# A hybrid attention layer on one core: the first gate-up product on the token halves' difference moved ahead of the last tile's differences, and a shorter chain for the inverse norms

## The chip, the core and the metric

The kernel runs on one core of a Trainium2 chip. The metric is the device time of one execution in microseconds (us), the median of several executions. The engines are named as in the profile: PE multiplies matrices, with its weight loads shown apart as PEld; DVE, ACT and POOL work elementwise; SP issues the DMAs. Each engine takes its instructions in the order in which they stand in its queue.

## What is computed

The program is one layer: a norm and an input projection, two kinds of attention side by side (NSA heads and HGRN2 heads), an output projection with the residual, then a second norm and a SwiGLU feed-forward block. The change touches the seam between the output projection and the feed-forward block:

```python
x = x + mix @ w_out[l]
h = rms_norm(x, norm_ffn[l])
gate, up = jnp.split(h @ w_gate_up[l], 2, axis=-1)
x = x + (jax.nn.silu(gate) * up) @ w_down[l]
```

There are 1024 tokens, in eight tiles of 128, and 1024 features; the feed-forward block is 2816 wide.

## The kernel before

Each float32 product is made of three matmuls: both operands are split in a high part (a copy on ACT, line 111) and a low part (a subtraction on DVE, line 112), and lines 118 to 120 multiply high by high, high by low and low by high. `product` splits one operand, a 128x512 page of weights, and runs the twelve matmuls against an `operand` that stands ready.

An `operand` tile is made by four transposes on PE into one PSUM bank (line 724), a copy on ACT (line 727) and a subtraction on DVE (line 728). The banks of these tiles come from `bank_s`, which has four: the fifth tile's transposes wait until DVE has read the first.

The gate-up stage multiplies by a scheme with seven block products in place of eight. Tokens are in two halves (tiles 0 to 3 and 4 to 7), features in two halves, gate and up columns in two. The scheme needs sums and differences of blocks. For the tokens, `pair_a(t)` makes the operands `b22` and `t1o` (`t1o` is the difference of the halves, already subtracted by line 748, and for the last tile by line 981), `pair_d(t)` makes three further differences `d` (lines 987 to 989, on POOL, the first of the last tile on DVE), and `pair_b(t)` turns them into the operands `t2o`, `t3o` and `t4o`. For the weights of block f, `gate_up_s1` adds two pages, `s1 = a[1,0] + a[1,1]` (line 972, POOL), and takes a difference (line 973, POOL); `gate_up_b` multiplies `s1` by `t1o` (the product `q`), subtracts a page from `s1` (line 1012, POOL) and multiplies it by `t2o`, and so on through the pages; a further subtraction on POOL (line 1015) makes the page of its last product. `gate_up_a(0)` and `gate_up_a(1)`, the first two blocks' products on `b11` and `b21`, run ahead of that. The weight pages come by DMA through a ring of three slots of two pages each (`rpage`, line 708).

Before this seam the last output tile (token tile 7) is added to the residual (line 497), its squares are summed on ACT (line 242), and `norm_stats` makes the inverse root on DVE through `rsqrt` (lines 125 to 131): twelve instructions on a 128x1 column. Then line 743 scales x of tile 7. The other seven tiles went the same way earlier, during the attention stage.

The order of the instructions on each engine isn't the order of the code. A scheduler sets it when the program is built: of the instructions that its own model of the times holds ready it takes the one that stands first in the code. Two lines that change places in the code thus change who goes first where both are held ready, also on engines that the edit doesn't name, and another number of instructions on one engine can shift the interleaving from there on.

Of the kernel before, what the change touches and what calls it, by code (L numbers as in the profile page):

```python
# [8 lines left out]
F32 = mybir.dt.float32  # L9
F32R = mybir.dt.float32r  # L10
BF16 = mybir.dt.bfloat16
I32 = mybir.dt.int32
U8 = mybir.dt.uint8
AF = mybir.ActivationFunctionType
OP = mybir.AluOpType
# [3 lines left out]
P = 128  # L19
D = 1024  # L20
T = 1024
NT = T // P
# [10 lines left out]
EPS = 1e-6  # L33
# [15 lines left out]
def hybrid_layer(ctx: ExitStack, tc: tile.TileContext, x, x_t, par, w_in, k_norm, pos_k, pos_v,  # L49
                 ck_w1, ck_w2, cv_w1, cv_w2, w_out, norm_ffn, w_gu, w_down, cst, hmask, out):  # L50
    nc = tc.nc
    V, A, G, PE = nc.vector, nc.scalar, nc.gpsimd, nc.tensor

    const = ctx.enter_context(tc.tile_pool(name="const", bufs=1))
    small = ctx.enter_context(tc.tile_pool(name="small", bufs=2))
# [19 lines left out]
    def bank8():  # L75

        turn[0] = (turn[0] + 1) % 8
        return acc() if turn[0] < 2 else ps_t() if turn[0] < 4 else bank_s()
# [6 lines left out]
    def bank_s():  # L85
        return pool[0].tile([P, 512], F32, name="bank", tag="s", bufs=4)
# [21 lines left out]
    def split(hi, lo, src, gain=None):  # L108

        if gain is None:  # L110
            A.activation(hi, src, AF.Copy)  # L111
            V.tensor_tensor(lo, src, hi.bitcast(F32), op=OP.subtract)  # L112
        else:
            A.activation(hi, src, AF.Copy, scale=gain)
            V.scalar_tensor_tensor(lo, src, gain, hi.bitcast(F32), op0=OP.mult, op1=OP.subtract)

    def mm3(o, ah, al, bh, bl, first, last, chained=False):
        PE.matmul(o, ah, bh, start=first, stop=False, skip_group_check=chained)  # L118
        PE.matmul(o, ah, bl, start=False, stop=False, skip_group_check=chained)  # L119
        PE.matmul(o, al, bh, start=False, stop=last, skip_group_check=chained)  # L120

    def rsqrt(y, ss, n, scale, eps, parts=P):
        v = small.tile([P, 64], F32, name="rs_v", tag="rs_v")[:parts, :n]
        t = small.tile([P, 64], F32, name="rs_t", tag="rs_t")[:parts, :n]
        V.tensor_scalar(v, ss, scale, eps, op0=OP.mult, op1=OP.add)
        V.tensor_scalar(t.bitcast(I32), v.bitcast(I32), 1, None, op0=OP.logical_shift_right)
        V.tensor_scalar(y.bitcast(I32), t.bitcast(I32), -1, 0x5F3759DF, op0=OP.mult, op1=OP.add)
        for _ in range(3):
            V.tensor_tensor(t, y, y, op=OP.mult)
            V.scalar_tensor_tensor(t, t, -0.5, v, op0=OP.mult, op1=OP.mult)  # L130
            V.scalar_tensor_tensor(y, t, 1.5, y, op0=OP.add, op1=OP.mult)
# [105 lines left out]
        return lambda i: parts_of(f(i))  # L237

    def norm_stats(src, junk):
        ss = small.tile([P, 1], F32, name="n_ss", tag="n_ss")  # L240
        rs = small.tile([P, 1], F32, name="n_rs", tag="n_rs", bufs=NT)
        A.activation(junk, src, AF.Square, accum_out=ss)
        rsqrt(rs, ss, 1, 1.0 / D, EPS)
        return rs

# [463 lines left out]
    def product(src, op, w=None, o=None):  # L711
        o = bank8() if o is None else o
        w = wring.tile([P, 2, 512], F32R, name="wop", tag="w") if w is None else w
        split(w[:, 0], w[:, 1], src)
        for c in range(4):
            sl = slice(c * P, (c + 1) * P)
            mm3(o, w[:, 0, sl], w[:, 1, sl], op[:, 0, c], op[:, 1, c], c == 0, c == 3)
        return o
# [231 lines left out]
    b21, t2o, b22, t1o, t3o, t4o = (opA[:, 0], opA[:, 1], opB[:, 0], opB[:, 1], opC[:, 0], opC[:, 1])  # L950
# [18 lines left out]
    def gate_up_s1(f, a):  # L969

        s1 = tmp[:, 8 + f % 2] if f else ff.tile([P, 512], F32, name="s1", tag="d", bufs=6)
        G.tensor_tensor(s1, a[1, 0], a[1, 1], op=OP.add)  # L972
        G.tensor_tensor(a[1, 0], a[0, 0], a[1, 0], op=OP.subtract)
        return s1
# [3 lines left out]
    def pair_a(t):  # L978
        operand(b22, x1[:, t + 4, 512:1024], t, bank_s)
        if t == 3:  # L980
            V.tensor_tensor(x1[:, 7, 0:512], x1[:, 7, 0:512], x1[:, 3, 0:512], op=OP.subtract)
        operand(t1o, x1[:, t + 4, 0:512], t, bank_s)

    def pair_d(t):
        xa, xb = x1[:, t, :], x1[:, t + 4, :]
        d = dif[t] = [ff.tile([P, 512], F32, name=f"d{i}", tag="d", bufs=6) for i in range(3)]
        (G if t < 3 else V).tensor_tensor(d[0], xb[:, 512:1024], xb[:, 0:512], op=OP.subtract)
        G.tensor_tensor(d[1], d[0], xa[:, 0:512], op=OP.subtract)
        G.tensor_tensor(d[2], xa[:, 512:1024], d[0], op=OP.subtract)

    def pair_b(t):
        for i, op in enumerate((t2o, t3o, t4o)):
            operand(op, dif[t][i], t, bank_s)
# [3 lines left out]
    nxt = [gate_up_a(0), gate_up_a(1)]  # L997
    for t in range(3):
        pair_a(t)
    for t in range(3):  # L1000
        pair_d(t)
        pair_b(t)
    s1s = [gate_up_s1(0, nxt[0][0])]
    pair_a(3)
    pair_d(3)
    pair_b(3)
    tmp = big.tile([P, 16, 512], F32, name="tmp", tag="A1")

    def gate_up_b(f, a, s1):
        u2, c11, u3, c22 = (tmp[:, 4 * (f % 2) + i] for i in range(4))  # L1010
        q = product(s1, t1o)
        G.tensor_tensor(s1, s1, a[0, 0], op=OP.subtract)  # L1012
        V.tensor_tensor(u2, product(s1, t2o), u2, op=OP.add)
        act_later()
        G.tensor_tensor(a[0, 1], a[0, 1], s1, op=OP.subtract)
        V.tensor_tensor(u3, product(a[1, 0], t3o), u2, op=OP.add)
        act_later()
        V.tensor_tensor(c22, q, u3, op=OP.add)
        V.tensor_tensor(u2, q, u2, op=OP.add)
        V.tensor_tensor(u3, product(a[1, 1], t4o), u3, op=OP.add)  # L1020
        act_later()
        V.tensor_tensor(u2, product(a[0, 1], b22), u2, op=OP.add)
        act_later()
        i, kh = f // 2, f % 2
        for hf, (gt, up) in enumerate(((c11, u3), (u2, c22))):
            th = ff.tile([P, 512], F32, name="th", tag="d", bufs=6) if kh else tmp[:, 10 + 2 * (i % 2) + hf]
            A.activation(th, gt, AF.Tanh, scale=0.5)
            V.scalar_tensor_tensor(th, th, 1.0, gt, op0=OP.add, op1=OP.mult)
            V.scalar_tensor_tensor(th, th, 0.5, up, op0=OP.mult, op1=OP.mult)
            if (kh, hf) != (0, 1):  # L1030
                act_store({(0, 0): 0, (1, 0): 1, (1, 1): 5}[kh, hf], i, th)
            blk[kh, hf] = th
        if kh:
            later.extend(act_sums(i, dict(blk)))
# [5 lines left out]
    def act_store(k, i, src):  # L1040
        nc.sync.dma_start(act_d[(k * NH + i) * P:(k * NH + i + 1) * P, :], src)
# [27 lines left out]
    def act_later():  # L1069
        if later:  # L1070
            later.pop(0)()
# [214 lines left out]
```

## Time and profile before

| what | value |
|---|---|
| median of 3 runs | 1405.82 us (1403.95 to 1405.95) |
| the profiled execution | 1406.47 us, its span 1404.6 us |
| PE busy | 1371.6 us, 98% of the span |
| DVE busy | 1048.0 us, 75% |
| ACT busy | 596.5 us, 42% |
| POOL busy | 392.1 us, 28% |

The profiled execution is 0.65 us above the median. The span runs from the first to the last instruction; the rest of the time lies around it. PE's busy time counts overlapping, pipelined matmuls, so a busy PE isn't PE at its peak. Times of single instructions are counted from the start of the span. The attention stage ends near 750 us, the seam lies between 750 and 780 us, gate-up runs to about 1235 us, and the down projection to the end.

### The profile page before, as it was taken

To read this page: it belongs to the slowest core of one execution; us is meant where nothing else is said; L and a number is where in the kernel's file an instruction comes from. 1 tells how busy PE (TensorE), PEld (TensorE's weight loads), DVE (VectorE), ACT (ScalarE), POOL (GpSimd) and SP (SyncE) were. 2 spreads that over 40 slices of the span, in tenths; PEclk is the share of its full clock that TensorE was granted. 3 is DMA by queue.
4 is the path that set the end of the run, shared out by engine and by line. 5 is a ranking of instruction groups with operands and counts; after the bars stand their busy time and mean duration, and the time that the engine had idled before them with its cause. 6 is when DMAs were issued, how large, how long until landed. Compare 5 with 4: busy or idle time off the path is not lost.

```text
span 1404.6 us, 19716 instructions
## 1 busy us (share of the span) xinstructions
PE 1371.6 (98%) x7092; PEld 1129.5 (80%) x7092; DVE 1048.0 (75%) x1893; ACT 596.5 (42%) x1153; POOL 392.1 (28%) x341
## 2 busy tenths in 40 slices
PE   9999999999999999999998999999999999999998
PEld 7888888989977777777776888888888888887787
DVE  5317888626788888888877888888888887689764
ACT  7323333323446666566654433333333333443332
POOL 0001111010044442344436433233233230158400
PEclk9999999999999999999999999999999999999999
DMA  8411110111220001000003333333333328887521
GB/s 324 127 45 31 31 31 28 54 31 46 94 88 1 1 1 61 31 16 31 16 16 105 96 101 97 112 98 113 113 112 99 106 98 294 327 300 269 171 97 55
DMA packets 108769, 135.72 MB, mean 97 GB/s; under 512 B 6112, under 2 KB 63872, under 8 KB 108672
## 3 DMA queue, kind: packets, MB, share of 16 engines
q1 hardware_dynamic: 108672, 134.46, 28.7%
q8 instruction: 56, 0.92, 0.3%
q14 instruction: 41, 0.34, 0.1%
HBM read 105.87 MB, written 28.57 MB: 96 GB/s over the span
## 4 chain that ended last, share of the span: by engine, by line
PE 82%; DVE 12%; ACT 2%; issue 2%; POOL 1%; DMA 1%; SPq 0%; ACTq 0%; POOLq 0%; DVEq 0%
PE bank L118 9%; PE bank L119 9%; PE bank L120 9%; PE a L118 8%; PE a L120 8%; PE a L119 8%; PE ps_t L119 4%; PE ps_t L120 4%; PE ps_t L118 4%; PE ps_t L861 3%; PE a L865 2%; DVE wop L112 2%; PE a L866 2%; PE ps_t L375 1%; PE ps_s L839 1%
## 5 line engine op out<-in xcount | busy, mean ns | idle before, releaser
L850 POOL TENSOR_SCALAR pbig<-pbig,den,gates 128x640 f32<-128x640 f32 (+7 forms) x128 | 103.9, 816 | 166.9 <-DVE den L849 146.9
L111 ACT ACTIVATE wop<-rpage 128x512 fp32r<-128x512 f32 x132 | 82.7, 630 | 156.9 <-PE bank L120 70.7
L112 DVE TENSOR_TENSOR wop<-rpage,wop 128x512 fp32r<-128x512 f32 x132 | 100.7, 765 | 14.6 <-ACT wop L111 12.7
L864 DVE TENSOR_TENSOR ph<-ps_t,ph 128x512 fp32r<-128x512 f32 x126 | 84.3, 683 | 18.5 <-ACT ph L863 17.6
L863 ACT ACTIVATE ph<-ps_t 128x512 fp32r<-128x512 f32 x126 | 72.7, 596 | 49.6 <-PE ps_t L861 39.7
L381 POOL TENSOR_TENSOR kp<-kp,fp 128x256 f32<-128x256 f32 x28 | 20.3, 725 | 232.8 <-PE bank L358 181.3
L861 PE MATMUL ps_t<-ident,pbig 128*128 128x128 f32 x504 | 78.7, 275 | 2.1 <-POOL pbig L850 2.1
L112 DVE TENSOR_TENSOR wop<-act_a,wop 128x512 fp32r<-128x512 f32 x48 | 46.8, 976 | 33.1 <-ACT wop L111 33.1
L861 PEld LDWEIGHTS ps_t<-ident,pbig 128*128 128x128 f32 x504 | 61.0, 141 | 11.9 <-POOL pbig L850 3.2
L1012 POOL TENSOR_TENSOR tmp<-tmp,rpage 128x512 f32<-128x512 f32 x21 | 31.3, 1488 | 140.6 <-DVE wop L112 140.6
L112 DVE TENSOR_TENSOR wlo<-wraw,whi 128x1024 fp32r<-128x1024 f32 (+2 forms) x27 | 32.0, 1188 | 46.0 <-PE a L120 19.3
L848 ACT ACTIVATE pbig<-ps_s,nm 128x640 f32<-128x640 f32 (+3 forms) x64 | 55.9, 875 | 24.1 <-DVE nm L847 19.0
L111 ACT ACTIVATE wop<-act_a 128x512 fp32r<-128x512 f32 x48 | 30.3, 631 | 82.8 <-PE bank L120 58.0
L118 PE MATMUL bank<-wop 128*128 128x512 f32 x165 | 65.3, 396 | 0.1
L119 PE MATMUL bank<-wop 128*128 128x512 f32 x165 | 65.2, 395 | 0.0
L120 PE MATMUL bank<-wop 128*128 128x512 f32 x165 | 65.1, 394 | 0.0
L847 DVE TENSOR_REDUCE nm<-ps_s 128x1 f32<-128x640 f32 (+3 forms) x64 | 58.1, 913 | 4.7 <-PE ps_s L842 3.0
L865 PE MATMUL a<-ph,kv 128*128 128x512 f32 x132 | 58.8, 445 | 2.2 <-ACT ph L863 1.4
L866 PE MATMUL a<-ph,kv 128*128 128x512 f32 x132 | 57.5, 436 | 2.9 <-DVE ph L864 1.8
L112 DVE TENSOR_TENSOR wop<-tmp,wop 128x512 fp32r<-128x512 f32 x42 | 43.6, 1039 | 20.6 <-ACT wop L111 19.9
L972 POOL TENSOR_TENSOR tmp<-rpage 128x512 f32<-128x512 f32 x20 | 26.1, 1306 | 115.2 <-DMA rpage<-in_w_gate_up_dram 115.2
L111 ACT ACTIVATE wop<-tmp 128x512 fp32r<-128x512 f32 x42 | 26.6, 633 | 70.2 <-POOL tmp L1012 37.5
(458 smaller groups left out, 4454.2 us busy)
## 6 DMA issues: line engine op xcount, KB each, us to landing
rpage<-in_w_gate_up_dram SPq DMA_DIRECT2D x86, 256.0 KB, 3.1
raws<-in_w_down_dram SPq DMA_DIRECT2D x35, 512.0 KB, 7.5
act_a<-act_d SPq DMA_DIRECT2D x12, 1024.0 KB, 6.4
act_d<-as SPq DMA_DIRECT2D x33, 256.0 KB, 2.2
act_e<-act_d SPq DMA_DIRECT2D x6, 1024.0 KB, 7.6
act_d<-tmp SPq DMA_DIRECT2D x22, 256.0 KB, 2.1
act_d<-th SPq DMA_DIRECT2D x22, 256.0 KB, 2.1
xn<-in_x_dram SPq DMA_DIRECT2D x8, 512.0 KB, 5.5
```

The source lines that it names most:

```text
L111: A.activation(hi, src, AF.Copy)
L112: V.tensor_tensor(lo, src, hi.bitcast(F32), op=OP.subtract)
L118: PE.matmul(o, ah, bh, start=first, stop=False, skip_group_check=chained)
L119: PE.matmul(o, ah, bl, start=False, stop=False, skip_group_check=chained)
L120: PE.matmul(o, al, bh, start=False, stop=last, skip_group_check=chained)
L847: V.tensor_reduce(nm, sv, axis=AX.XY, op=OP.max, negate=True)
L850: G.tensor_scalar(pp, pp, den, gates[:, qb, h * 3 + 1 + b:h * 3 + 2 + b], op0=OP.mult, op1=OP.mult)
L861: PE.transpose(pt[:, r * P:(r + 1) * P], wts[r][:, c0:c0 + P], ident)
L863: A.activation(ph[:, 0], pt, AF.Copy)
L864: V.tensor_tensor(ph[:, 1], pt, ph[:, 0].bitcast(F32), op=OP.subtract)
L865: PE.matmul(o, vst[b][:, kb, g, :], ph[:, 0], start=b == 0 and kb == kb0, stop=False)
L866: PE.matmul(o, vst[b][:, kb, g, :], ph[:, 1], start=False, stop=False)
```

## The change

Two edits. In `norm_stats` the chain is written out with the factor -0.5 taken into a column `h` once, so that one round of the iteration is two instructions in place of three: ten instructions in place of twelve, with four small tiles. In the seam, `gate_up_s1(0)` stands ahead of the loop over `pair_d` and `pair_b` instead of behind it, and the product `q` of block 0 is issued between `pair_d(3)` and `pair_b(3)`, into a bank of `bank_s`; `gate_up_b` takes it from there.

```diff
     def norm_stats(src, junk):
-        ss = small.tile([P, 1], F32, name="n_ss", tag="n_ss")
-        rs = small.tile([P, 1], F32, name="n_rs", tag="n_rs", bufs=NT)
+        ss, v, h, t = (small.tile([P, 1], F32, name=n, tag=n) for n in ("n_ss", "n_v", "n_h", "n_t"))
+        y = small.tile([P, 1], F32, name="n_rs", tag="n_rs", bufs=NT)
         A.activation(junk, src, AF.Square, accum_out=ss)
-        rsqrt(rs, ss, 1, 1.0 / D, EPS)
-        return rs
+        V.tensor_scalar(v, ss, 1.0 / D, EPS, op0=OP.mult, op1=OP.add)
+        V.tensor_scalar(t.bitcast(I32), v.bitcast(I32), 1, None, op0=OP.logical_shift_right)
+        V.tensor_scalar(y.bitcast(I32), t.bitcast(I32), -1, 0x5F3759DF, op0=OP.mult, op1=OP.add)
+        V.tensor_scalar(h, v, -0.5, None, op0=OP.mult)
+        for _ in range(3):
+            V.scalar_tensor_tensor(t, y, y, h, op0=OP.mult, op1=OP.mult)
+            V.scalar_tensor_tensor(y, t, 1.5, y, op0=OP.add, op1=OP.mult)
+        return y
...
     for t in range(3):
         pair_a(t)
+    s1s = [gate_up_s1(0, nxt[0][0])]
     for t in range(3):
         pair_d(t)
         pair_b(t)
-    s1s = [gate_up_s1(0, nxt[0][0])]
     pair_a(3)
     pair_d(3)
+    q_first = [product(s1s[0], t1o, o=bank_s())]
     pair_b(3)
...
-        q = product(s1, t1o)
+        q = q_first.pop() if q_first else product(s1, t1o)
```

The diff moves more than its lines. Behind the edit each line of the code stands six or seven lines lower: 972 is 978, 987 to 989 are 993 to 995, 1012 is 1019, 727 is 733, 724 is 730.

On POOL, at the seam, before (`s_7716` is `s1`, the `d` are the differences of `pair_d`, three for each tile):

```order
L987 TENSOR_TENSOR d_7635<-x_3322 128x512
L988 TENSOR_TENSOR d_7636<-d_7635,x_3322 128x512
L989 TENSOR_TENSOR d_7637<-x_3322,d_7635 128x512
L987 TENSOR_TENSOR d_7662<-x_3322 128x512
L988 TENSOR_TENSOR d_7663<-d_7662,x_3322 128x512
L989 TENSOR_TENSOR d_7664<-x_3322,d_7662 128x512
L987 TENSOR_TENSOR d_7689<-x_3322 128x512
L988 TENSOR_TENSOR d_7690<-d_7689,x_3322 128x512
L989 TENSOR_TENSOR d_7691<-x_3322,d_7689 128x512
L972 TENSOR_TENSOR s_7716<-rpage 128x512
```

And now, the first ten on POOL at the same place:

```order
L978 TENSOR_TENSOR s_7627<-rpage 128x512
L993 TENSOR_TENSOR d_7630<-x_3322 128x512
L979 TENSOR_TENSOR rpage<-rpage 128x512
L994 TENSOR_TENSOR d_7631<-d_7630,x_3322 128x512
L995 TENSOR_TENSOR d_7632<-x_3322,d_7630 128x512
L993 TENSOR_TENSOR d_7657<-x_3322 128x512
L1019 TENSOR_TENSOR s_7627<-s_7627,rpage 128x512
L994 TENSOR_TENSOR d_7658<-d_7657,x_3322 128x512
L1022 TENSOR_TENSOR rpage<-rpage,s_7627 128x512
L995 TENSOR_TENSOR d_7659<-x_3322,d_7657 128x512
```

The sum of the two weight pages went from the tenth place to the first, and the other three instructions on block 0's weights stand between the differences; the three differences of tile 2 and the last two of tile 3 follow as eleventh to fifteenth.

On ACT, behind the copies of the operand tiles of `pair_a(0)` to `pair_a(2)`, before (`wop` is the split of a weight page, line 111; `opA` and `opC` are operand tiles, line 727):

```order
L727 ACTIVATE opB<-bank 128x4x128 x6
L727 ACTIVATE opA<-bank 128x4x128
L727 ACTIVATE opC<-bank 128x4x128 x2
L111 ACTIVATE wop<-rpage 128x512
L111 ACTIVATE wop<-epage 128x512
L727 ACTIVATE opA<-bank 128x4x128
L111 ACTIVATE wop<-s_7716 128x512
L727 ACTIVATE opC<-bank 128x4x128 x2
```

And now:

```order
L733 ACTIVATE opB<-bank 128x4x128 x6
L111 ACTIVATE wop<-rpage 128x512
L111 ACTIVATE wop<-epage 128x512
L111 ACTIVATE wop<-s_7627 128x512 x2
L111 ACTIVATE wop<-rpage 128x512 x3
L733 ACTIVATE opA<-bank 128x4x128
L733 ACTIVATE opC<-bank 128x4x128 x2
```

All seven splits of block 0's and block 1's first pages stand ahead of the first copy of a difference tile; on DVE the subtractions stand in the same order. The second split of `s` reads what line 1019 writes, and the last of the three `rpage` reads what line 1022 writes.

On PE, behind the 32 transposes of `b21`, `b22` and `t1o`, before came five tiles of differences, then the 24 matmuls of the first two blocks. Now it reads, from the end of those 24:

```order
L120 MATMUL a_7569<-opA,wop 128x512
L730 MATMUL bank<-ident,d_7630 128x128 x4
L730 MATMUL bank<-ident,d_7631 128x128 x4
L730 MATMUL bank<-ident,d_7632 128x128 x4
L730 MATMUL bank<-ident,d_7657 128x128 x4
L730 MATMUL bank<-ident,d_7658 128x128 x4
L730 MATMUL bank<-ident,d_7659 128x128 x4
L730 MATMUL bank<-ident,d_7684 128x128 x4
L730 MATMUL bank<-ident,d_7685 128x128 x4
L730 MATMUL bank<-ident,d_7686 128x128 x4
L730 MATMUL bank<-ident,x_3322 128x128 x8
L118 MATMUL bank<-opB,wop 128x512
```

The 24 matmuls come first and all nine tiles of differences after them, then the two tiles of `pair_a(3)` and the twelve matmuls of `q`; behind these stand the three tiles of `pair_b(3)`, and then seven matmuls of the product on `b22`, ahead of the product on `t2o`.

## Rows read from the trace of the kernel before

**Rows 1.** Busy time by stretch: PE, PEld, DVE, ACT, POOL (instructions), clock, DMA share, GB/s.

```profile
750.00:760.00 10.00, 6.55 (x47) 4.64 (x44) 9.21 (x21) 8.30 (x16) 7.75 (x7) 1.00 0.76 210
760.00:770.00 10.00, 8.61 (x45) 6.62 (x46) 9.85 (x15) 3.12 (x8) 5.09 (x4) 1.00 0.18 52
770.00:780.00 10.00, 8.40 (x45) 6.59 (x46) 8.40 (x15) 7.72 (x16) 6.44 (x6) 1.00 0.01 3
...
850.00:950.00 100.00, 100.00 (x443) 82.83 (x442) 81.99 (x103) 32.23 (x53) 30.48 (x21) 1.00 0.31 96
```

**Rows 2.** PE in time order at the seam: start, us, [idle before <- releaser].

```profile
753.25 0.63 PE L724 MATMUL bank<-ident,x 128*128 128x128 f32 x4 [0.90 <-DVE opA L728]
...
767.86 1.91 PE L724 MATMUL bank<-ident,d 128*128 128x128 f32 x16
...
772.76 0.66 PE L724 MATMUL bank<-ident,d 128*128 128x128 f32 x4 [1.03 <-POOL d L988]
773.99 0.66 PE L724 MATMUL bank<-ident,d 128*128 128x128 f32 x4 [0.57 <-POOL d L989]
774.40 0.47 PE L118 MATMUL bank<-opB,wop 128*128 128x512 f32 x1
```

**Rows 3.** POOL in time order at the seam.

```profile
747.01 1.31 POOL L987 TENSOR_TENSOR d<-x 128x512 f32<-128x512 f32 x1
...
753.46 1.27 POOL L989 TENSOR_TENSOR d<-x,d 128x512 f32<-128x512 f32 x1
...
760.63 1.29 POOL L972 TENSOR_TENSOR s<-rpage 128x512 f32<-128x512 f32 x1
...
768.52 1.59 POOL L1012 TENSOR_TENSOR s<-s,rpage 128x512 f32<-128x512 f32 x1 [4.83 <-DVE wop L112]
...
772.65 1.28 POOL L989 TENSOR_TENSOR d<-x,d 128x512 f32<-128x512 f32 x1
```

**Rows 4.** The weight pages of block 0: first issue, time to landing, DMA by stretch.

```profile
751.46 0.74 SPq L708 DMA_DIRECT2D rpage<-in_w_gate_up_dram  x1
...
rpage<-in_w_gate_up_dram SPq DMA_DIRECT2D x4, 256.0 KB, 5.8
...
758.00:759.00 1.00, 0.26 (x4) 0.17 (x3) 1.00 (x3) 0.87 (x3) 0.92 (x2) 1.00 0.90 222
759.00:760.00 1.00, 0.48 (x4) 0.25 (x3) 1.00 (x3) 1.00 (x3) 1.00 (x2) 1.00 0.01 2
```

**Rows 5.** DVE: the chain's last instructions by tile (min/median/max ns), and two tiles' subtractions.

```profile
L131 DVE SCALAR_TENSOR_TENSOR n_rs<-rs_t,n_rs x24: 141/159/973, 590.8 to 761.2; 128x1 f32<-128x1 f32 x24
...
770.33 1.28 DVE L728 TENSOR_TENSOR opC<-bank,opC 128x512 fp32r<-128x512 f32 x2
```

**Rows 6.** ACT in time order: the first two splits of weight pages.

```profile
758.87 0.63 ACT L111 ACTIVATE wop<-rpage 128x512 fp32r<-128x512 f32 x1
759.40 0.61 ACT L111 ACTIVATE wop<-epage 128x512 fp32r<-128x512 f32 x1
```

**Rows 7.** Two stretches in which the granted clock (third value from the right) fell.

```profile
561.00:562.00 1.00, 0.72 (x3) 0.72 (x4) 1.00 (x2) 0.23 (x2) 0.37 (x1) 0.78 0.00 0
...
564.00:565.00 1.00, 1.00 (x6) 0.82 (x5) 1.00 (x2) 0.00 (x0) 0.75 (x1) 0.51 0.00 0
...
1302.00:1303.00 1.00, 0.00 (x0) 0.00 (x0) 1.00 (x2) 0.00 (x0) 1.00 (x2) 0.63 0.63 37
...
1309.00:1310.00 1.00, 1.00 (x5) 0.81 (x5) 0.67 (x1) 0.00 (x0) 0.00 (x0) 0.96 0.38 143
```

**Rows 8.** PE's waits by releaser (total, times, longest): 590 to 746, then 780 on.

```profile
PE ps_s L839 <- ACT pbig L848: 2.0, 3, 0.7
PE a L866 <- DVE ph L864: 1.8, 5, 0.4
PE a L866 <- DVE rs_t L129: 0.6, 1, 0.6
...
PE ps_t L119 <- DVE wop L112: 3.5, 4, 2.4
```

## The prediction, made before the changed kernel ran

> **What bounds the kernel now.** I read the busy time by stretch first. PE is busy 98% of the span, and through gate-up it never waits: 443 matmuls in 100 us, 0.226 us each, from 850 to 950 us, and the next two stretches of that length read alike [rows 1]. The seam is different. Between 750 and 780 us PE is idle for 30 - 6.55 - 8.61 - 8.40 = 6.4 us, while DVE is nearly full [rows 1]. PE's own rows say why. In the first part its transposes wait for a bank that DVE has to empty (0.90 us at 753.25); at the end they wait for POOL's last two differences, 1.03 and 0.57 us; from 774.40 on it runs through [rows 2]. So what the seam gains or loses reaches the end in full, unless the later stages take some of it up.
>
> **The sum of the weight pages at the head of POOL's queue.** This decides the forecast. Before, POOL began the differences at 747.01, right behind its work for the last tiles, and came to the sum at 760.63 [rows 3]. Now the sum is POOL's first instruction there, and it needs two pages of block 0. Their DMAs are not moved: the first of four is issued at 751.46, the four take 5.8 us in the median, and the DMA engines are at 0.90 from 758 to 759 us and at 0.01 in the next microsecond [rows 4]. So the last of these pages lands near 759.0. POOL, which has work at 747, stands until then, with fourteen instructions behind the sum. Its pace is 1.29 us: from 747.01 to 753.46 are five of them [rows 3]. I count from 759.0: the first, second, sixth, seventh, ninth and thirteenth end at 760.3, 761.6, 766.7, 768.0, 770.6 and 775.8.
>
> PE comes to it as follows. The 32 transposes end near 755.4, as before. Then stand the 24 matmuls, whose first page ACT can split only when it has landed; before, the two splits started at 758.87 and 759.40 [rows 6]. So PE starts them near 758.9 and, at 0.226 us each, ends near 764.5. Four tiles of differences follow, as POOL makes them, to 767.2 (the fourth is POOL's sixth instruction). The fifth needs a bank. No bank is emptied, since ACT and DVE hold the splits ahead of the tiles' copies: the second split of s waits for POOL's seventh, and the last of the three pages for POOL's ninth, at 770.6. That split ends at 771.2, the first copy at 771.8, and DVE empties the first bank by 772.4. **PE thus stands from about 767 to 772.5.**
>
> From there DVE empties a tile in 0.60 to 0.64 us [rows 5]. Nine tiles from 771.8 would be done at 777.3, but the ninth is POOL's thirteenth (775.8): transposes to 776.3 (16 take 1.91 us, so four about half a microsecond [rows 2]), copy to 776.9, subtraction to 777.5. The two tiles of pair_a(3) behind it are ready at 778.6, and q's twelve matmuls run to 781.3. The first difference of tile 3 is made on DVE by 779.2, the other two on POOL by 781.9, their transposes end at 782.4. The same work was done before at 774.40 + 12 x 0.226 = 777.1 [rows 2]: before, q's matmuls were the last of it. **The term is 782.4 - 777.1 = +5.3 us.** What the edit is built on is there: q's 2.7 us do cover POOL's two differences of tile 3, on which PE waited 1.6 us. But they are covered five microseconds later. If POOL ran at the 1.59 us that line 1012 took [rows 3], the twelve instructions from the second to the thirteenth would add up to 12 x 0.30 = 3.6 us; DVE has little to do while POOL catches up, so I add nothing and leave part of this to the range.
>
> **A second wait behind it.** After that point PE has seven matmuls of the b22 product (1.6 us, to 784.0), and then needs the t2o tile of tile 3. Its copy on ACT stands behind a split of block 1's s, which waits for POOL's sixteenth instruction: 781.9 + 1.3 = 783.2, split to 783.8, a tanh to 784.3, the copy to 784.9, DVE to 785.5. **+1.5 us**; it is nothing if POOL and ACT make up that time, so its bounds are 0 and 1.5.
>
> **The clock.** After PE's waits near 560 us the granted clock is under 1 in four slices of a microsecond, from 0.78 to 0.51, and around the wait at 1300 to 1303 us in eight, from 0.63 to 0.96, with 0.50 between [rows 7]. That is the lower level, 1.2 of 2.4 GHz. The work done there at half speed, some 3.2 and 6.9 us, cost 1.6 and 3.4 us. In the seam of before the clock held at 1.00, with PE busy 6.55 of 10 us [rows 1]. Now PE has a gap without any work of 3.4 us and one of over 5; the wait before the fall at 1302 us was 2.4 us [rows 8]. What the first costs is hidden, since PE has to wait at 767 anyway. After the second come q and what follows. I take the cheaper incident, **+1.6 us**, since the sparse transposes from 772 on may raise the clock again ahead of q; bounds 0 and 3.4. The Trainium skill ("TensorE: Matmul & The Clock Gate", Part 1: The HAM clock gate) says that an idle PE drops to 1.2 GHz and sustained activity lets it back, which the two places of this trace agree with. By it alone the term would be of the dearer kind, as the gap is longer than either, and the time 1.8 us higher.
>
> **The shorter chain.** Two instructions of twelve go, for each of eight tiles, and POOL stands while the last chain runs. One such instruction takes 159 ns in the median and up to 973 [rows 5]. For tile 7 the chain and the scaling behind it end near 758.5 instead of 764.8, but nobody waits for that: the transposes of tile 7 stand behind all differences on PE. I count nothing for it here. In the attention stage DVE saves 7 x 2 instructions, some 2 us, off the path but for the 0.6 us that PE waited there for the chain [rows 8]. The order of the whole stage from about 590 us on is shuffled, though; PE's waits in it are 2.0 + 1.8 + 0.6 = 4.4 us [rows 8], and I take -0.6, with -4.4 and +4.4 as bounds.
>
> **The sum**: 5.3 + 1.5 + 1.6 - 0.6 = +7.8 us. On the profiled execution's 1406.47 us that is 1414.3; it is 0.65 us above the median of the runs, so the forecast is 1413.6 us, 0.55% slower. All bounds together are +0.9 and +14.6 (1406.7 and 1420.4).
>
> **Rivals.** *It does what its name says.* If the pages were there when POOL reaches the sum, the differences would be made as early as before, q would fill PE's 1.6 us, and with the shorter chain half of the other 4.8 us of PE's idle time in the seam could go: -4.0 us, 1401.8. It decides by the landing: the sum would have to start 6.8 us sooner than 759.0, at 752, for the change to cost nothing. Against it: the first of the four DMAs is issued only at 751.46 [rows 4]. Chance 0.06.
>
> *The loss is given back.* From 1290 to 1310 us PE waits 3.5 us for DVE's splits [rows 8], and the half clock costs another 3.4 [rows 7]. If that stage is set by DMAs and POOL and not by when PE comes, a PE that is late waits less: 1413.6 - 6.9 = 1406.7, no change. For it: DVE and POOL have their own queue there. Against it: their pages come through slots that gate-up frees, so they are late as well. Chance 0.10.
>
> *The shuffled attention stage* costs as much again as PE's waits in it, 4.4 us, instead of 0.6 less: 1413.6 + 5.0 = 1418.6. For it: the scheduler's model also let the sum go first. Chance 0.09.
>
> **How the numbers follow.** The forecast has 0.75, from 1409 to 1418. A measurement of this kernel can tell about 0.2% (2.8 us) from no change. The first rival is faster, the second within that, the forecast and the third slower: 0.06, 0.10, 0.84. The range of 1408.0 to 1418.8 leaves out the first two rivals and little else.
>
> **What would show it.** In the trace of after: POOL idle from about 747 to 759 us, released by the DMA of a weight page, and the differences only then; ACT's second split of s released by line 1019; PE with a gap of about five microseconds that ends with DVE's first difference tile; q's matmuls near 778.6 instead of 774.4; the clock at 0.5 around there. I am wrong if POOL's sum starts before 752 us, if the copies of difference tiles go ahead of the splits, or if PE's later waits shrink by what the seam loses.

## The result: 1.4% slower, more than twice the forecast loss

The changed kernel takes 1423.76 us in the median of four runs (1422.99 to 1424.61), the kernel before 1404.88 (1403.46 to 1405.95). The ratio is 1.0143, with an interval of 1.0131 to 1.0155: about 19 to 20 us lost where 7.8 were forecast. At the seam the sign and the mechanism were right and the size was not; the attention stage, forecast to gain a little, lost. 1423.76 lies 5 us above the end of the range.

The busy time by stretch shows where PE stands now; it answers to [rows 1] (the columns are those named there).

```profile
750.00:760.00 10.00, 8.12 (x53) 6.34 (x51) 7.33 (x19) 6.46 (x12) 0.27 (x1) 1.00 0.62 172
760.00:770.00 10.00, 6.14 (x17) 4.87 (x18) 7.07 (x9) 1.78 (x3) 5.53 (x4) 0.66 0.51 145
770.00:780.00 10.00, 3.85 (x25) 3.01 (x23) 4.71 (x4) 4.15 (x8) 9.92 (x8) 0.95 0.05 15
780.00:790.00 10.00, 6.57 (x33) 5.88 (x34) 8.93 (x13) 3.99 (x8) 4.00 (x4) 0.71 0.30 90
790.00:800.00 10.00, 7.31 (x37) 5.68 (x36) 5.86 (x7) 4.27 (x9) 9.84 (x8) 1.00 0.01 2
850.00:950.00 100.00, 100.00 (x443) 82.81 (x442) 84.99 (x107) 32.21 (x52) 29.30 (x20) 1.00 0.33 107
```

Between 760 and 780 us PE is busy 10 of 20 us, and it is not through with the seam before 800. POOL, which was busy 7.75 us of 750 to 760 before [rows 1], is busy 0.27 us there now. Gate-up behind it is untouched: 443 matmuls in 100 us, as before. PE's own rows say for what it waits (start, us, [idle before <- releaser]), to be held against [rows 2]:

```profile
757.32 2.02 PE L730 MATMUL bank<-ident,x 128*128 128x128 f32 x12 [0.89 <-DVE n_t L248]
763.86 0.80 PE L118 MATMUL a<-opA,wop 128*128 128x512 f32 x1 [4.52 <-ACT wop L111]
...
773.42 0.66 PE L730 MATMUL bank<-ident,d 128*128 128x128 f32 x4 [0.23 <-POOL d L993]
782.12 4.17 PE L730 MATMUL bank<-ident,d 128*128 128x128 f32 x20 [8.04 <-DVE opA L734]
786.13 1.04 PE L730 MATMUL bank<-ident,x 128*128 128x128 f32 x8
787.96 0.50 PE L118 MATMUL bank<-opB,wop 128*128 128x512 f32 x1 [0.79 <-ACT opB L733]
788.97 0.50 PE L119 MATMUL bank<-opB,wop 128*128 128x512 f32 x1 [0.51 <-DVE opB L734]
...
797.66 0.50 PE L118 MATMUL bank<-opA,wop 128*128 128x512 f32 x1 [2.19 <-DVE opA L734]
```

The gap for a bank is there, 8.04 us long; it was forecast at 5.5. The product q, in the rows 787.96 and 788.97, comes 13.56 us later than before (774.40, [rows 2]). The chain behind the gap reads from POOL to ACT to DVE. POOL first, against [rows 3]:

```profile
748.99 1.29 POOL L754 TENSOR_TENSOR x<-x 128x512 f32<-128x512 f32 x1
764.47 1.80 POOL L978 TENSOR_TENSOR s<-rpage 128x512 f32<-128x512 f32 x1 [14.20 <-DMA rpage<-in_w_gate_up_dram]
...
773.33 1.26 POOL L1019 TENSOR_TENSOR s<-s,rpage 128x512 f32<-128x512 f32 x1
...
775.78 1.71 POOL L1022 TENSOR_TENSOR rpage<-rpage,s 128x512 f32<-128x512 f32 x1
```

POOL stands 14.20 us for the page. Then ACT, which holds the splits (line 111) ahead of the first copy of a difference tile (line 733), the last row here:

```profile
763.17 0.63 ACT L111 ACTIVATE wop<-rpage 128x512 fp32r<-128x512 f32 x1 [3.20 <-DMA rpage<-in_w_gate_up_dram]
...
774.62 0.63 ACT L111 ACTIVATE wop<-s 128x512 fp32r<-128x512 f32 x1 [7.69 <-POOL s L1019]
775.16 1.13 ACT L111 ACTIVATE wop<-rpage 128x512 fp32r<-128x512 f32 x2
777.52 0.63 ACT L111 ACTIVATE wop<-rpage 128x512 fp32r<-128x512 f32 x1 [1.23 <-POOL rpage L1022]
778.06 0.58 ACT L733 ACTIVATE opA<-bank 128x512 fp32r<-128x512 f32 x1
```

And DVE, which finishes each split before it empties the first bank (the last row):

```profile
775.29 1.08 DVE L112 TENSOR_TENSOR wop<-s,wop 128x512 fp32r<-128x512 f32 x1 [6.78 <-ACT wop L111]
776.29 5.08 DVE L112 TENSOR_TENSOR wop<-rpage,wop 128x512 fp32r<-128x512 f32 x3
781.30 0.68 DVE L734 TENSOR_TENSOR opA<-bank,opA 128x512 fp32r<-128x512 f32 x1
```

Three splits take 5.08 us there. In the forecast one took 0.6.

### The profile page after: what moved, and what is told of

Its sections match the earlier page's. It is cut to its first block, busy times and chain, and to the rows that moved or that the text cites. A ratio compares the mean times of both kernels' runs of the same rounds, so it can differ in the third digit from the quotient of the medians.

```text
span 1421.8 us, 19688 instructions
## 1 busy us (share of the span) xinstructions
PE 1373.9 (97%) x7092; PEld 1130.9 (80%) x7092; DVE 1054.1 (74%) x1877; ACT 596.6 (42%) x1153; POOL 396.2 (28%) x341
## 4 chain that ended last, share of the span: by engine, by line
PE 81%; DVE 11%; ACT 3%; issue 2%; POOL 1%; DMA 1%; SPq 0%; ACTq 0%; POOLq 0%; DVEq 0%
PE bank L120 9%; PE bank L118 9%; PE bank L119 9%; PE a L120 8%; PE a L118 8%; PE a L119 8%; PE ps_t L119 4%; PE ps_t L120 4%; PE ps_t L118 4%; PE ps_t L867 3%; PE a L871 2%; DVE wop L112 2%; PE a L872 2%; PE ps_t L381 1%; DVE nm L853 1%
## 5 line engine op out<-in xcount | busy, mean ns | idle before, releaser
L112 DVE TENSOR_TENSOR wop<-rpage,wop 128x512 fp32r<-128x512 f32 x132 | 107.0, 812 | 16.1 <-ACT wop L111 14.2
L118 PE MATMUL bank<-wop 128*128 128x512 f32 x154 | 60.4, 392 | 0.0
L119 PE MATMUL bank<-wop 128*128 128x512 f32 x154 | 60.4, 392 | 0.0
L120 PE MATMUL bank<-wop 128*128 128x512 f32 x154 | 60.2, 391 | 0.0
L118 PE MATMUL a<-whi,hT_h 128*128 128x256 f32 (+2 forms) x168 | 55.2, 328 | 0.0
```

## The loss in two stretches

The seam isn't the whole of it. Three anchors are the same work in every kernel: DVE's first output tile of the NSA heads in the attention stage, PE's first transposes at the seam, and the last of PE's long waits in the down projection. In the kernel before they stand at 572.41, 745.80 and 1303.02 us. In the trace of after the first, on DVE, reads

```profile
571.16 0.69 DVE L503 TENSOR_TENSOR x<-a,x 128x512 f32<-128x512 f32 x1
```

and the other two, on PE,

```profile
749.89 1.04 PE L730 MATMUL bank<-ident,x 128*128 128x128 f32 x8
...
1322.02 0.80 PE L119 MATMUL ps_t<-wop 128*128 128x512 f32 x1 [2.38 <-DVE wop L112]
```

So the attention part takes 178.73 us instead of 173.39 (+5.34), and from the seam to the last wait it is 572.13 instead of 557.22 (+14.91). The rest lies outside both: the profiled execution came 1.25 us sooner to the first anchor, and from the last anchor to the end it needs 99.78 us instead of 101.58. The sum is 5.34 + 14.91 - 1.25 - 1.80 = 17.2 us, the difference of the two spans (1421.8 and 1404.6).

Those last two terms go with falls of the granted clock that one execution has and another lacks, or has for a shorter time. A stretch ahead of the first anchor and the one around the last, by the busy time (the third value from the right is the clock), in the kernel before:

```profile
424.00:430.00 6.00, 5.79 (x29) 4.84 (x29) 3.93 (x12) 3.84 (x14) 4.03 (x8) 0.72 0.02 4
...
1302.00:1310.00 8.00, 6.98 (x18) 5.53 (x19) 6.32 (x8) 0.00 (x0) 2.10 (x2) 0.57 0.64 197
```

And the same work in the changed kernel:

```profile
424.00:430.00 6.00, 5.79 (x40) 4.91 (x40) 4.36 (x14) 4.97 (x16) 4.18 (x8) 1.00 0.02 4
...
1321.00:1329.00 8.00, 6.98 (x24) 5.66 (x25) 7.01 (x10) 1.33 (x3) 2.10 (x2) 0.79 0.56 197
```

PE is as busy, but before it did 29 matmuls in the time of 40, and 18 in that of 24. Up to the first anchor all the kernels below run the same order; the executions of e2, e3 and e7 have the first fall too (0.72), the other nine have not. So the first fall is no effect of an edit. The one around the last anchor is absent in e4, e6 and e9, and no pattern by edit shows in it. The anchors thus measure more finely here than the spans do.

All kernels by these anchors (attention: first to second; seam: second to third, less the 557.22 us of before), beside the ratio of the times and its interval:

| kernel | attention, us | seam, us | ratio |
|---|---|---|---|
| before | 173.39 | 0 | 1 |
| changed | 178.73 | +14.91 | 1.0143 (1.0131 to 1.0155) |
| e1, chain only | 178.74 | +1.63 | 1.0055 (1.0042 to 1.0068) |
| e2, seam's edit only | 173.51 | +16.71 | 1.0106 (1.0090 to 1.0123) |
| e3, q only | 173.41 | +0.75 | 1.0000 (0.9991 to 1.0009) |
| e4, sum only | 173.41 | +17.11 | 1.0111 (1.0095 to 1.0128) |
| e5, chain of tile 7 only | 173.43 | +1.78 | 1.0013 (1.0005 to 1.0022) |
| e6, sum without pages | 173.44 | +0.29 | 0.9996 (0.9987 to 1.0005) |
| e7, no differences of tile 2 | 173.40 | +15.36 | 1.0118 (1.0102 to 1.0133) |
| e8, one tile ahead of the sum | 173.35 | +11.92 | 1.0085 (1.0071 to 1.0098) |
| e9, all differences on POOL | 173.45 | -0.03 | 0.9999 (0.9988 to 1.0009) |
| e10, e9 with q | 173.51 | +0.90 | 0.9998 (0.9990 to 1.0007) |
| e11, fewer differences | 173.49 | +8.92 | 1.0066 (1.0051 to 1.0080) |
| e12, chain padded | 173.82 | +0.66 | 1.0013 (1.0003 to 1.0023) |

Each row is one execution. The eleven kernels with the old order in the attention stage have 173.35 to 173.51 us in the attention part, so that column is good to about 0.2 us. The seam's column has no such repeat, and falls of the clock between the second and the third anchor are in it: the kernel before, e3 and e9 have none there, all the others have.

## Experiments: which edit, and which half of it

**e1, the chain alone.** The `norm_stats` of the change; the seam as before.

> Only the ten-instruction chain; the seam stands as before. Theory A: in the changed kernel the seam's work already began 4.1 us late (transposes of the token tiles at 749.89 instead of 745.80 us), and that is the chain's doing, since the attention stage was put in another order by it. Then this kernel loses about 4 us: +3 to +5 us, a ratio of 1.002 to 1.0035, and PE reaches those transposes near 749.9 us. Theory B: the 4.1 us come from the seam's edit or from chance, and the chain is worth what its saved instructions say: 0 to -2 us, transposes at 745.8 us or sooner.

It lost 0.55%, more than either theory had. The attention part is 178.74 us, so the 5.3 us are the chain's: theory A. (They look like 3.9, and in the changed kernel like 4.1, at the second anchor because of the clock's fall near 425 us, which this execution and that of after lack.) The rest, 1.63 us, is at the seam. In the order with the short chain ACT has both splits of `s` ahead of two copies, and PE waits for the bank that these should empty. ACT's rows:

```profile
772.68 0.63 ACT L111 ACTIVATE wop<-s 128x512 fp32r<-128x512 f32 x1 [4.87 <-POOL s L1018]
773.22 1.07 ACT L733 ACTIVATE opC<-bank 128x512 fp32r<-128x512 f32 x2
```

And PE's:

```profile
775.62 1.09 PE L730 MATMUL bank<-ident,d 128*128 128x128 f32 x4 [2.93 <-DVE opC L734]
```

It is the mechanism of the changed seam on a small scale: a split that waits for POOL, and behind it the copies that free PE's banks. The clock fell there too, to 0.79 in the mean from 772 to 780 us; how the wait and the clock share the 1.63 us isn't parted.

**e2, the seam's edit alone**, with the chain of twelve.

> Only the seam's edit, with the old chain of twelve. Theory A: everything but the 4.1 us of the attention stage stays, so the loss is 18.9 - 4.1 = about +14.8 us (ratio 1.0095 to 1.0115), PE starts the 24 matmuls near 759.8 us, at half clock, stands about 8 us for the bank of a difference tile, and starts q near 783.9 us. Theory B (the two edits work together, the short chain brings the splits ahead of the copies): under +8 us.

As theory A had it: 1.06%, the 24 matmuls at 758.21 us and q at 782.44, an execution in which the second anchor is at 744.51. Only the gap for the bank was shorter than the 8 us expected, 6.26 us; PE stood another 1.46 us for POOL's first difference, among the 24 matmuls. The two edits do their harm apart: 5.3 and 16.7 us by the anchors, against 5.3 and 14.9 in the changed kernel. (In e2 the clock also fell from 793 to 797 us, which it did not in the changed kernel.)

**e3 and e4 part the seam's edit**, both with the old chain, as do e6, e7, e8 and e11 below; the code shown is what each changes against e2. e3 keeps `q_first` and puts the sum back in its old place; e4 moves the sum and leaves q.

```diff
+    for t in range(3):
+        pair_d(t)
+        pair_b(t)
     s1s = [gate_up_s1(0, nxt[0][0])]
-    for t in range(3):
-        pair_d(t)
-        pair_b(t)
```

> The product q of block 0 is issued between the differences and the operands of tile 3, with the old chain, but the sum of the weight pages stays where it was, so that it is POOL's tenth instruction at the seam. Theory A: the whole loss of the seam belongs to the sum, and q alone does what the name of the change says: it covers some of the 1.6 us that PE waited for the last two differences: -0.5 to -2 us (ratio 0.9985 to 0.9997). Theory B: issuing q early costs by itself, since it holds a bank of the four: +2 us or more.

```diff
-    q_first = [product(s1s[0], t1o, o=bank_s())]
...
-        q = q_first.pop() if q_first else product(s1, t1o)
+        q = product(s1, t1o)
```

> The sum of the weight pages is moved ahead (POOL's first instruction at the seam), with the old chain, but q stands where it stood before. Theory A: nearly all of the seam's loss comes back, +13 to +17 us (ratio 1.009 to 1.012), and it is at least as slow as the seam's edit with q, because the last two differences are not covered. Theory B: under +5 us.

The whole loss is the sum's: 1.11% without q at all. And q alone gives nothing (1.0000), where at least 0.5 us was expected. Its trace says where the gain went. PE does not wait for the last two differences any more; it waits for two other things in their place:

```profile
770.05 0.50 PE L118 MATMUL bank<-opB,wop 128*128 128x512 f32 x1 [0.98 <-ACT opB L727]
...
776.11 0.50 PE L120 MATMUL bank<-opA,wop 128*128 128x512 f32 x1 [1.06 <-DVE wop L112]
```

The first is q's own operand, the copy of token tile 3 that PE now reaches too soon, the second the split of `s` for the product behind it. 1.60 us of waiting became 2.04. What the edit is named for was not there to be had.

## Experiments: why the sum's place costs so much

**e6, the pages taken out of the sum.**

```diff
         s1 = tmp[:, 8 + f % 2] if f else ff.tile([P, 512], F32, name="s1", tag="d", bufs=6)
+        if f == 0:
+            G.tensor_tensor(s1, x1[:, 0, 0:512], x1[:, 1, 0:512], op=OP.add)
+            return s1
```

> The seam's edit with the old chain, but the sum of block 0 adds two columns of x that have long been in memory instead of two pages that a DMA brings, and the difference on the second page is left out (so block 0's s and one page are other numbers). Theory A: the sum's place at the head of POOL's queue costs only because its pages land near 759 us; without that wait POOL begins the differences right behind it, near 749 us, and the loss of +14.9 us falls to between -2 and +2 us (ratio 0.9985 to 1.0015). Theory B: being first, ahead of the differences, costs by itself: +5 us or more.

Theory A: 0.9996. The sum is still POOL's first instruction there, at 744.99 us, and the differences follow it at once. The scheduler also orders ACT otherwise without the pages (the copies go ahead of the second split of `s`), and POOL has one instruction less, so this run shows that the wait and what hangs on it cost everything, not how much each does.

**e8, the sum behind the differences of tile 0.**

```diff
+    for t in range(1):
+        pair_d(t)
+        pair_b(t)
     s1s = [gate_up_s1(0, nxt[0][0])]
-    for t in range(3):
+    for t in range(1, 3):
         pair_d(t)
         pair_b(t)
```

> The seam's edit with the old chain, but the sum stands behind the differences of token tile 0: POOL's fourth instruction instead of its first. Theory A: POOL makes three differences in the time in which it stood, the sum starts no later (near 759 to 760 us), and all that follows comes three instructions, some 4 to 5 us, sooner; ACT's copies of difference tiles still wait for the second split of s. Loss +5 to +10 us. Theory B (the place in the queue matters only as first or not first): 0 to +2 us. Theory C (what costs is q's or the splits' place, not the sum's): +13 us or more.

The loss is 0.85%, +11.9 us by the anchors, in none of the three ranges. Theory A had the right half: the sum starts no later. But the copies aren't released by the sum. POOL's rows:

```profile
757.18 1.67 POOL L972 TENSOR_TENSOR s<-rpage 128x512 f32<-128x512 f32 x1 [8.69 <-DMA rpage<-in_w_gate_up_dram]
...
768.69 1.26 POOL L1016 TENSOR_TENSOR s<-s,rpage 128x512 f32<-128x512 f32 x1
```

ACT's:

```profile
769.99 0.63 ACT L111 ACTIVATE wop<-s 128x512 fp32r<-128x512 f32 x1 [10.47 <-POOL s L1016]
...
771.04 0.58 ACT L727 ACTIVATE opA<-bank 128x512 fp32r<-128x512 f32 x1
```

The subtraction that the second split of `s` needs (line 1016 here) is the eighth instruction from the sum on, as in e2, and the copies begin 27.7 us behind the second anchor (771.04 - 743.37) as they do in e2 (772.27 - 744.51 = 27.8). The three differences that POOL made in the time gained only save work behind the gap. What decides is POOL's subtraction on `s`, for which ACT's second split of `s` stands; the forecast had this step, but as one of several.

**e7 and e11, POOL with less to do.** e7 leaves out the three differences of tile 2, e11 the third of tile 1 too.

```diff
         xa, xb = x1[:, t, :], x1[:, t + 4, :]
+        if t == 2:
+            dif[t] = [xb[:, 0:512], xa[:, 0:512], xa[:, 512:1024]]
+            return
...
-        G.tensor_tensor(d[2], xa[:, 512:1024], d[0], op=OP.subtract)
+        if t == 1:
+            d[2] = xa[:, 512:1024]
+        else:
+            G.tensor_tensor(d[2], xa[:, 512:1024], d[0], op=OP.subtract)
```

> The seam's edit with the old chain, but the three differences of token tile 2 are not made: the transposes read columns of x instead. The order on PE, DVE and ACT is the same, row for row; POOL has three instructions fewer, just while DVE makes the last three splits. Theory A: in the changed kernel these three subtractions took 5.08 us instead of 3 x 0.68 because POOL worked on memory beside them; here they take about 0.7 us each once POOL has made the page of the last one, PE's gap for the bank shrinks by 1.5 to 3 us, and the loss is +11 to +13.5 us instead of +14.9. Theory B: DVE's subtractions are slow for a reason of their own: still 1.7 us each, and +14 to +16 us.

> The seam's edit with the old chain, the three differences of token tile 2 and the third of tile 1 left out (the transposes read columns of x instead): POOL then has nothing to do from the last page's subtraction on. Some rows behind the gap change places. With the tile 2 differences alone left out, the three last splits took 2.95 us in place of 4.02, while POOL's third difference of tile 1 ran beside the first of them. Theory A (DVE is slowed by what POOL does beside it): all three splits now in 2.0 to 2.2 us, and PE's gap for the bank ends another 0.7 to 1 us sooner after the first transposes of the seam: 30.2 to 30.6 us instead of 31.2. Theory B: they stay near 2.95 us. For the time +13 to +16 us by both, since the two readings differ by less than the runs resolve.

First e2. POOL's differences in the gap:

```profile
773.73 1.71 POOL L987 TENSOR_TENSOR d<-x 128x512 f32<-128x512 f32 x1
...
777.07 1.27 POOL L989 TENSOR_TENSOR d<-x,d 128x512 f32<-128x512 f32 x1
```

DVE beside them (line 112 reads a page and its high part, both in memory; line 728 a bank):

```profile
771.96 4.02 DVE L112 TENSOR_TENSOR wop<-rpage,wop 128x512 fp32r<-128x512 f32 x3
...
776.50 1.27 DVE L728 TENSOR_TENSOR opC<-bank,opC 128x512 fp32r<-128x512 f32 x2
```

The same three splits on DVE in e7:

```profile
772.31 2.95 DVE L112 TENSOR_TENSOR wop<-rpage,wop 128x512 fp32r<-128x512 f32 x3
```

In e11 two of them, with tile 3's first difference (line 990) between; POOL is idle from 770.54 to 772.44 us:

```profile
771.02 0.68 DVE L112 TENSOR_TENSOR wop<-rpage,wop 128x512 fp32r<-128x512 f32 x1
771.62 0.68 DVE L990 TENSOR_TENSOR d<-x 128x512 f32<-128x512 f32 x1
772.22 0.68 DVE L112 TENSOR_TENSOR wop<-rpage,wop 128x512 fp32r<-128x512 f32 x1
```

So the splits are slow because of POOL: 1.3 us each in e2 and 1.7 in the changed kernel, 0.6 to 0.7 with POOL idle. The time answered less clearly. e7's gap for the bank is only 0.5 us shorter (5.75 us, where e2 has 6.26), by the anchors it saved 1.35 us, and its ratio, 1.0118, can't be told from e2's 1.0106: not the +11 to +13.5 us expected, since POOL's third difference of tile 1 still ran beside the splits. e11 has the expected length to the gap's end (773.65 - 743.42 = 30.2 us), but loses only 0.66%, far less than the +13 to +16 us expected. Only two of the three splits stand ahead of the gap's end, the third comes at 783.17 us; DVE makes tile 3's first difference in its place, in the same 0.68 us, POOL's last two end at 775.26 us, q starts 35.9 us behind the second anchor instead of 37.9, and the waits of 0.5 and 2.2 us behind q are gone. Up to 1.6 of these 7.8 us are the clock's fall from 793 to 797 us, which e2 and e7 have and e11 lacks. How much of the rest is the collision and how much the four instructions that POOL lacks, e11 can't say, since rows changed places.

**e9 and e10, another way to the two waits.** POOL stood 4.83 us in the kernel before [rows 3]; e9 gives it tile 3's first difference, e10 adds q.

```diff
-        (G if t < 3 else V).tensor_tensor(d[0], xb[:, 512:1024], xb[:, 0:512], op=OP.subtract)
+        G.tensor_tensor(d[0], xb[:, 512:1024], xb[:, 0:512], op=OP.subtract)
```

> The kernel before with one letter changed: the first difference of token tile 3 is made on POOL like the others, not on DVE. The order on PE and ACT is untouched, DVE has one instruction less, and on POOL the three differences of tile 3 stand around the subtraction of line 1012 instead of behind line 1015. Theory A: POOL stood 4.83 us ahead of that subtraction, so the last two differences come 1.3 us or more sooner and PE's waits of 1.03 and 0.57 us for them shrink: -0.5 to -1.6 us (ratio 0.9988 to 0.9997). Theory B: PE then waits for something else at the same place (the split of s, the copies of the last tiles), as it did when q was put there: -0.3 to +0.5 us.

> As the run before, and q of block 0 issued between the differences and the operands of tile 3, with the sum in its old place and the old chain. With q alone the 1.6 us of waiting became 0.98 us for the copy of tile 3 that q reads and 1.06 us for the second split of s: a ratio of 1.000. Theory A (the seam is held by several chains of about the same length): again nothing, 0.999 to 1.001. Theory B (POOL was the last of them): -1 to -2.5 us (0.998 to 0.9993).

Nothing, twice: 0.9999 and 0.9998. In e9 the wait for the first of the differences falls from 1.03 to 0.28 us, but the other 0.57 us stay, now for a bank that DVE empties, and by the anchors the kernel ends as it did. The seam of the kernel before is held by several chains of nearly one length. No kernel here is faster than the one before.

## Experiments: why a shorter chain costs five microseconds

**e5** gives the short chain to token tile 7 alone (`norm_stats(..., t == NT - 1)`), so that the attention stage keeps the old order. **e12** gives it to all eight and puts two copies between its steps (the code against the changed kernel):

```diff
+            if _ < 2:
+                V.tensor_scalar(t, y, 1.0, None, op0=OP.mult)
+                V.scalar_tensor_tensor(t, t, y, h, op0=OP.mult, op1=OP.mult)
+            else:
+                V.scalar_tensor_tensor(t, y, y, h, op0=OP.mult, op1=OP.mult)
-            V.scalar_tensor_tensor(t, y, y, h, op0=OP.mult, op1=OP.mult)
```

> The ten-instruction chain for token tile 7 alone; the other seven tiles keep twelve, so that the attention stage runs in the order of before. The chain alone cost 7.7 us. Theory A: 5.4 us of it are the other order of the attention stage (from the first output tile to the transposes of the seam 178.7 us instead of 173.4), and the rest is the seam, where ACT now holds both splits of the sum ahead of two copies (PE waits 2.9 us for that bank at 775.6 us). Then this kernel starts the seam's transposes as early as before and loses +1.5 to +3.5 us (ratio 1.001 to 1.0025). Theory B: the whole loss is the attention stage, and a shorter chain in front of the seam helps there: 0 to -2 us.

> The short chain of all eight tiles with two copies of a 128x1 column put between its steps, twelve instructions as before, ten of them those of the change; the seam stands as before. The scheduler gives the attention stage a third order: on PE 912 of 6974 rows stand elsewhere than in the kernel before (1097 with the short chain alone). So far every kernel with the old order took 173.4 us from the first output tile to the seam, and both kernels with the short chain 178.7. Theory A: the order sets that time, not the chain; a third order gives a third time, at least 0.7 us from both. Theory B: the short chain itself is what costs (or saves too little), whatever the order: 178.0 to 179.0 us again. Theory C: the two instructions that are missing decide, since DVE's work then meets other work: with twelve it is 173.4 again.

e5 is theory A: 173.43 us in the attention part, +1.78 at the seam, 1.0013. The chain in front of the seam gains nothing there; through the order of ACT it costs, with a wait of 3.19 us for the bank as in e1. The clock fell there as well (0.79 from 768 to 776 us), so this 1.78 isn't the wait's alone either.

e12 lies between its theories: 173.82 us, another value than both, but only 0.43 from the old one, where theory A asked for 0.7. Theory B falls: the short chain's own steps are in it, and 4.9 of the 5.3 us are not. Whether those went with the order (912 rows on PE differ from before) or with the number of instructions, e12 doesn't part. What the 5.3 us consist of, the traces show. The busy time of the attention part in the kernel before:

```profile
572.41:745.80 173.39, 167.93 (x942) 130.41 (x941) 139.70 (x310) 108.86 (x211) 69.75 (x58) 1.00 0.06 24
```

In the changed kernel:

```profile
571.16:749.89 178.73, 170.38 (x943) 130.62 (x942) 138.03 (x296) 108.77 (x211) 71.07 (x58) 1.00 0.06 23
```

In e12:

```profile
569.78:743.60 173.82, 168.54 (x942) 130.53 (x941) 137.04 (x310) 108.36 (x211) 70.67 (x58) 1.00 0.06 24
```

From the first to the second, PE's idle time grew from 5.46 to 8.35 us, and the same matmuls, at the full clock, were busy 2.45 us longer, so they overlapped less. DVE did save 1.67 us. In e12 both are nearly back. PE's longest waits there in the changed kernel, to be held against [rows 8] (total, times, longest):

```profile
PE ps_s L845 <- ACT pbig L854: 3.1, 7, 0.9
PE a L872 <- DVE ph L870: 1.7, 6, 0.6
PE a L120 <- DVE rpage L517: 1.3, 2, 0.9
PE a L871 <- ACT ph L869: 0.7, 2, 0.4
```

More waits for ACT's `pbig`, and a new one for the split of a product's operand (line 517): by these rows the work on PE's queue mixes less well. Why the new order does that is not shown.

## Why the prediction was wrong

By its own steps, with 4.09 us (749.89 - 745.80) taken off each time of after, so that both seams begin together:

| step | forecast | measured, less 4.09 |
|---|---|---|
| transposes of the first tiles end on PE | 755.4 | 755.2 |
| the 24 matmuls | 758.9 to 764.5 | 759.8 to 767.6 |
| the sum starts on POOL | 759.0 | 760.4 |
| POOL's seventh and ninth end | 768.0, 770.6 | 770.5, 773.4 |
| last split ends on ACT | 771.2 | 774.1 |
| DVE has emptied the first bank | 772.4 | 777.9 |
| q's matmuls start | 778.6 | 783.9 |
| transposes of tile 3's differences end | 782.4 | 789.0 |

**The sum at the head of POOL's queue** was read rightly, and each sign named for it came, q's matmuls later than said: POOL idle until a DMA of a weight page, the second split of `s` released by line 1019, one long gap ended by DVE's first difference tile, the clock at half. The term was mis-sized, with its clock: up to the last row of the table 789.0 - 777.1 = 11.9 us, where 5.3 and 1.6 for the clock were forecast.

**The step that failed most is the pace.** I took 1.29 us for each of POOL's instructions and 0.6 for each of DVE's splits, durations of rows in which the other engine happened to be doing something else. I saw the row of 1.59 us, worked out 3.6 us from it, and added nothing. POOL's nine instructions took 13.02 us from 764.47 on, 1.45 each, and DVE's last three splits 5.08 us: 2.8 and 2.6 of the 5.5 us by which the first bank came late (the first with the sum's later start of 1.4 in it). e7 and e11 show the cause of DVE's part. POOL's own rows show its part: the first three took 1.73 to 1.80 us beside DVE's subtractions, the next five 1.26 to 1.28 with DVE idle. Why the sum's pages landed 1.4 us later than forecast is not shown.

**The clock** fell twice, as the gaps suggested. The first fall, on the 24 matmuls, cost nothing, since PE had to wait behind them. In the second PE ran the transposes at 1.2 of 2.4 GHz from 782.12 us: the stretch from 782 to 786 has a clock of 0.52 (the third value from the right):

```profile
782.00:786.00 4.00, 3.88 (x19) 3.91 (x20) 3.57 (x6) 1.99 (x4) 1.74 (x2) 0.52 0.44 131
```

I had put the cheaper of two incidents there (1.6 us), and the rows bear that size out: 20 transposes took 4.17 us, where 16 took 1.91 at the full clock [rows 2], so 20 would have taken about 2.4, or 3.0 at DVE's pace of 0.6 a tile. By this estimate 1.2 to 1.8 us went, so the 5.0 us by which the term and its clock were missed are the pace's and the sum's later start's.

**The second wait** was 2.19 us and 0.51 for another tile, together 2.7 instead of 1.5.

**The shorter chain** was the other failure: -0.6 forecast, 5.34 measured in the attention stage, outside the bounds of 4.4 either way. The bound was the sum of PE's waits; here they grew by 2.89 us, which it allows, and the same matmuls were busy 2.45 us longer, which it left out. The rival that had this stage cost more got a chance of 0.09.

**The other rivals.** *As its name says* asked for a sum before 752 us; e6 gives it that (with other numbers in `s`), and e3 q without the sum: 0.9996 and 1.0000, so even then no 4 us were to be gained. *The loss is given back* is refuted: the waits from 1290 us on are 3.5 us again, one for one.

So the sum of the misses is: attention 5.9, the seam's term with its clock 5.0, the second wait 1.2, together 12.1 us on 7.8: 19.9, against a median of +18.9.

## What to carry to other kernels

Where a scheduler fills the queues in the order of the code, moving a line moves it on every engine, and the instruction to look at is not the one that was moved for a purpose but the first that needs something not there yet: all behind it in that queue waits too, and whoever waits for those. Price such a jam with durations from rows in which both engines work at once, and bound an edit that renumbers a long stretch by more than the waits that are in it. Before covering a wait with other work, look what that work itself waits for; here it was a wait of the same length.

## What the runs showed of the hardware

DVE and POOL slow each other when DVE's subtraction reads both operands from memory: 0.68 us alone, up to 1.76 with POOL at work, and POOL's 1.27 becomes 1.7. When DVE reads a bank, neither is slowed: in e2 two subtractions of line 728 took 1.27 us together from 776.50 on, beside POOL's 1.27 at 777.07. The Trainium skill ("SBUF — State Buffer", section "SBUF: two separate sides") says that a DVE operation with two inputs in SBUF and a GpSimd operation that reads it take a shared pair of ports by turns, as an exclusive lock for the whole instruction. The trace agrees on who is slowed and when. By a strict lock a pair would take 0.68 + 1.27 = 1.95 us, or 1.83 by the starts of back-to-back rows, 0.60 and 1.23 apart; in e2 POOL's third and fourth instructions started 1.68 us apart (761.65 and 763.33), so a little of the two overlaps, and the measurement decides.

The clock fell and rose in stretches that no edit touched, in some executions and not in others (near 425 us in four of the fourteen profiles, and around the last anchor for different lengths, or not at all). One such fall moves the end by 1 to 2 us, as much as several of the effects looked for here.
